# The closing step of a feed-forward: two weight units by token tiles in place of four

## The chip, the cores and the metric

One NeuronCore of one Trainium2 chip. The metric is the device time of one execution in microseconds; lower is better.

## The reference, cut to what matters

A block of two layers, each a mixer and a feed-forward with layer norms, is followed by a second block of another kind. The change touches the feed-forward of both layers of the first block; the second block's input is a modulated form of what the second layer leaves.

```
for l in range(2):
    x = layer_norm(ALPHA * x + mixed, ln1_g[l], ln1_b[l])
    ff = jnp.square(jax.nn.relu(x @ w_up[l])) @ w_down[l]
    x = layer_norm(ALPHA * x + ff, ln2_g[l], ln2_b[l])
...
h = rmsnorm(x, pre_norm_mix) * (1.0 + scale_m) + shift_m
```

x has 256 tokens of 1024 columns, `w_up` is 1024 x 4096, `w_down` 4096 x 1024, all float32.

## The kernel before, in words

The 256 tokens are two token tiles of 128. A weight comes in units of 1 MB. `weight` (from L241) loads a unit from memory into one of two `raw` buffers through the queue of SP (L249); ACT copies it, rounded, into `hi` (L255) and DVE writes the rest, `raw` minus `hi`, into `lo` (L256), in pieces of 1024 columns where nothing else is said. There are four buffers of `hi` and four of `lo`. A `raw` buffer is free again after its last `lo`, a `hi`/`lo` pair after the last matmul that reads it. Each product is three matmuls on PE, hi x hi, hi x lo and lo x hi (`mm3`, L261 to L263).

`layer` holds the feed-forward. `up(j)` computes a block of 512 of the 4096 hidden columns from two units, squares its positive part and splits it into two halves, `hs[j]`. The loop over j then adds the product of `hs[j]` with the `down` units 2j and 2j+1 to four accumulators in PSUM, two token tiles by two halves of 512 columns, with `down` (L285), one unit at a time and both token tiles under it. One `up` runs ahead of it, and in each pass a part of the modulation (`modulation_part`: transfers of `ada` and eight products on DVE, L779), which the second block needs.

The last blocks are done otherwise, so that token tile 0 is ready before tile 1. `downs` (L292) takes several units for one token tile: all but the last unit for both column halves, then the last unit for the first half and for the second. Behind it `close` (L644) does the layer norm of that token tile on DVE: the sum with x (L652), statistics (L329, L331), the root by POOL (L309) and small column work (L310 to L316), the normalized x (L360, L362). In the first layer `split_t` turns x by PE transposes (L340) into `xT` (L345 on ACT, L346 on DVE), which the next layer's mixer reads: its first matmuls are those of `conv_in`, token tile by token tile (L261 to L263, 128x256), with a bias row that SP loads (L474). In the second layer `close` is followed by `modulated` (from L887): a sum of squares on ACT (L892), a scaling on DVE (L896), transposes on PE, gain and shift on DVE and ACT (L905, L903), and the split into `xT`. The second block's first projection (128x496, 24 matmuls a token tile) and two units of a gate (48 matmuls a token tile) read that. `modulation_end`, ahead of the second layer's closing step, sums the modulation parts on PE (L792), finishes them on DVE (L795, L798) and turns them by a PE transpose (L800).

The code gives no order across engines. A scheduler writes, when the program is built, one fixed order for each engine and for the queue of SP; each of them works through its own in turn.

Of the kernel before, what the change touches and what calls it, by code (L numbers as in the profile page):

```python
# [198 lines left out]
class Kernel:  # L199
# [500 lines left out]
    def layer(self, l):  # L700
        nc, vec, act, a = self.nc, self.nc.vector, self.nc.scalar, self.a
        order, ws = self.mixer_ops(l)

        g, b = self.row(a["ln1_g"], D * l), self.row(a["ln1_b"], D * l)
        xT = self.pair("xT", [128, KD, S])
        for t in range(NT):
            acc = [self.acc(), self.acc()]
            self.downs(acc, [(self.mixT, (2 * i, 2 * i + 1)) for i in order], ws, t)
            self.close(t, acc, None, g, b, xT)
        self.dump(f"x1_{l}", self.x[0])  # L710


        def relu2(p, shape):
            r = self.new("t2", shape)
            act.activation(r, p, AF.Relu)
            vec.tensor_tensor(out=r, in0=r, in1=p, op=OP.mult)
            return r

        def up(j):
            h = self.new("mh", [128, 2, 4, S], F32R)  # L720
            ws = [self.weight("up", l, 2 * j + u) for u in range(2)]
            if j == 0:
                for t in range(NT):
                    p = self.mm((128, 512))
                    for u in range(2):
                        self.tok_unit(ws[u], xT, p[:, 256 * u:256 * u + 256], t)
                    self.split_t(relu2(p, [128, 512]), (h[:, 0], h[:, 1]), 0, t)
            else:
                for u in range(2):
                    p = self.mm()  # L730
                    self.ws_unit(ws[u], xT, p)
                    self.split(h[:, 0, 2 * u:2 * u + 2, :], h[:, 1, 2 * u:2 * u + 2, :], relu2(p, [128, 2, 256]))
            return h[:, 0], h[:, 1]

        acc = [[self.acc(), self.acc()] for _ in range(NT)]
        hs = [up(0)]
        for j in range(6):
            hs.append(up(j + 1))
            self.modulation_part(6 * l + j)
            for i in range(2):  # L740
                w = self.weight("down", l, 2 * j + i)
                for t in range(NT):
                    self.down(acc[t], hs[j], (2 * i, 2 * i + 1), w, t, j == 0 and i == 0, False)
        hs.append(up(7))
        g, b = self.row(a["ln2_g"], D * l), self.row(a["ln2_b"], D * l)
        last = l + 1 == DEPTH
        if last:
            self.modulation_end()
        self.xT = self.pair("xT", [128, KD, S])
        ws = [self.weight("down", l, 12 + i) for i in range(4)]  # L750
        for t in range(NT):
            self.downs(acc[t], [(hs[6 + i // 2], (2 * (i % 2), 2 * (i % 2) + 1)) for i in range(4)], ws, t, False)
            self.close(t, acc[t], ALPHA, g, b, None if last else self.xT)
            if last:
                self.modulated(t, 0, 8, self.xT)
        self.dump(f"x2_{l}", self.x[0])
# [659 lines left out]
```

## Time and profile before

| | us |
|---|---|
| runs, lowest / median / highest | 1262.32 / 1267.88 / 1270.29 |
| the profiled execution | 1262.89 |
| its span, first to last instruction | 1261.1 |

The mean granted clock of TensorE over the span is 0.990 of full speed. Times in the rows are counted from the start of the span. PE is TensorE, DVE is VectorE, ACT is ScalarE, POOL is GpSimd, SPq is the queue of SyncE. In a timeline a row is: start, length, engine, line, operation, output and inputs, count; in brackets the idle time of that engine just before, and what ended it. Matmuls are pipelined, so the length of one is more than its distance to the next.

### The profile page before, as it was taken

How to read it: one execution, taken by the hardware profiler on the slowest of the kernel's cores; microseconds unless marked ns; L12 is line 12 of the kernel's file. 1: busy time of each engine (PE TensorE's matmuls, PEld its weight loads, DVE VectorE, ACT ScalarE, POOL GpSimd, SP SyncE). 2: the span in 40 equal slices, each digit the busy share in tenths (PEclk: the TensorE clock that was granted, in tenths of full speed). 3: DMA queues.
4: the chain of work that ended last, by engine and by line, in shares of the span. 5: the costliest groups of instructions: out<-in, count | busy, mean ns of one | idle time of the engine just before them, and what ended most of it. 6: DMA issues, size and time to landing. Idle time of an engine off the chain costs nothing.

```text
span 1261.1 us, 20407 instructions
## 1 busy us (share of the span) xinstructions
PE 1197.4 (95%) x8047; PEld 1061.4 (84%) x8047; DVE 939.6 (75%) x1655; ACT 684.3 (54%) x1178; POOL 37.6 (3%) x60
## 2 busy tenths in 40 slices
PE   6997989999999799999998899999999999999997
PEld 5985679899888578899977688799989978899996
DVE  5998587777899767877868974379988887655553
ACT  4546764434454775444435677667767645444341
POOL 2100000000000000000000000000000000000000
PEclk9999899999999999999999999999999999999999
DMA  8743567777652547787644444255654444555450
GB/s 309 264 148 136 177 234 256 258 290 263 223 219 92 183 150 252 272 286 276 246 163 169 148 169 156 79 201 201 214 187 170 165 168 144 191 201 192 178 199 34
DMA packets 53423, 247.80 MB, mean 196 GB/s; under 512 B 5276, under 2 KB 17596, under 8 KB 30544
## 3 DMA queue, kind: packets, MB, share of 16 engines
q1 hardware_dynamic: 52256, 243.22, 54.0%
q0 software_dynamic: 1072, 3.28, 0.8%
q8 instruction: 63, 1.03, 0.3%
q14 instruction: 32, 0.26, 0.1%
HBM read 241.06 MB, written 6.47 MB: 196 GB/s over the span
## 4 chain that ended last, share of the span: by engine, by line
PE 47%; DVE 23%; DMA 18%; ACT 6%; issue 4%; SPq 0%; POOL 0%; DVEq 0%; ACTq 0%; POOLq 0%
DMA raw<-in_wts 10%; PE mm L263 8%; PE mm L262 8%; PE mm L261 8%; DVE lo L256 8%; DMA s<-in_ada 6%; PE acc L263 5%; PE acc L261 5%; PE acc L262 5%; DVE cy L512 3%; ACT hi L255 3%; DVE t L779 3%; DMA rel<-reld 2%; DVE mask L1022 1%; PE tr L340 1%
## 5 line engine op out<-in xcount | busy, mean ns | idle before, releaser
L256 DVE TENSOR_TENSOR lo<-raw,hi 128x1024 fp32r<-128x1024 f32 (+1 forms) x367 | 430.8, 1185 | 172.4 <-ACT hi L255 171.9
L255 ACT ACTIVATE hi<-raw 128x1024 fp32r<-128x1024 f32 (+1 forms) x367 | 367.2, 1025 | 343.3 <-DMA raw<-in_wts 184.5
L261 PE MATMUL mm<-xT,hi 128*128 128x256 f32 x992 | 281.4, 284 | 0.0
L263 PE MATMUL mm<-xT,lo 128*128 128x256 f32 x992 | 281.0, 283 | 0.0
L262 PE MATMUL mm<-xT,hi 128*128 128x256 f32 x992 | 281.0, 283 | 0.0
L261 PEld LDWEIGHTS mm<-xT,hi 128*128 128x128 f32 x992 | 190.3, 192 | 0.9 <-issue 0.2
L262 PEld LDWEIGHTS mm<-xT,hi 128*128 128x128 f32 x992 | 190.2, 192 | 0.8
L263 PEld LDWEIGHTS mm<-xT,lo 128*128 128x128 f32 x992 | 190.2, 192 | 0.1
L261 PE MATMUL acc<-hi,mh 128*128 128x512 f32 x320 | 128.5, 401 | 5.3 <-ACT mh L599 5.3
L263 PE MATMUL acc<-hi,mh 128*128 128x512 f32 x320 | 126.8, 397 | 0.3 <-DVE mh L346 0.3
L262 PE MATMUL acc<-lo,mh 128*128 128x512 f32 x320 | 126.9, 396 | 0.0
L262 PE MATMUL mm<-lo,xT 128*128 128x256 f32 (+1 forms) x288 | 85.3, 296 | 2.1 <-DVE lo L256 2.1
L261 PE MATMUL mm<-hi,xT 128*128 128x256 f32 (+1 forms) x288 | 86.8, 301 | 0.6 <-ACT kmT L468 0.4
L263 PE MATMUL mm<-hi,xT 128*128 128x256 f32 (+1 forms) x288 | 85.7, 298 | 1.2 <-DVE xT L346 1.2
L779 DVE SCALAR_TENSOR_TENSOR t<-s,silu_c,t 128x512 f32<-128x512 f32 x84 | 62.8, 748 | 29.1 <-DMA s<-in_ada 28.7
L263 PE MATMUL mm<-h,lo 128*128 128x256 f32 x288 | 80.9, 281 | 0.0
L261 PE MATMUL mm<-h,hi 128*128 128x256 f32 x288 | 80.9, 281 | 0.0
L262 PE MATMUL mm<-h,hi 128*128 128x256 f32 x288 | 80.9, 281 | 0.0
L261 PEld LDWEIGHTS acc<-hi,mh 128*128 128x128 f32 x320 | 61.2, 191 | 19.3 <-ACT mh L599 6.1
L263 PEld LDWEIGHTS acc<-hi,mh 128*128 128x128 f32 x320 | 60.8, 190 | 14.7 <-issue 1.4
L262 PEld LDWEIGHTS acc<-lo,mh 128*128 128x128 f32 x320 | 61.2, 191 | 12.6 <-issue 1.1
L261 PEld LDWEIGHTS mm<-hi,xT 128*128 128x128 f32 x288 | 54.9, 191 | 5.7 <-issue 1.8
(386 smaller groups left out, 2179.9 us busy)
## 6 DMA issues: line engine op xcount, KB each, us to landing
raw<-in_wts SPq DMA_DIRECT2D x174, 1024.0 KB
s<-in_ada SPq DMA_DIRECT2D x48, 512.0 KB
rel<-reld SPq DMA_DIRECT2D x64, 64.0 KB
bias<-bo SPq DMA_DIRECT2D x16, 256.0 KB
bias<-bias SPq DMA_DIRECT2D x8, 512.0 KB
cr<-cumd SPq DMA_DIRECT2D x8, 512.0 KB
mh<-in_wts SPq DMA_DIRECT2D x3, 1024.0 KB
row<-in_ln_g SPq DMA_DIRECT2D x4, 512.0 KB
```

Source lines behind the costliest of these rows:

```text
L255: nc.scalar.activation(h[:, s], raw[:, s], AF.Copy)
L256: (lo_on or nc.vector).tensor_tensor(out=l[:, s], in0=raw[:, s], in1=h[:, s].bitcast(F32), op=OP.subtract)
L261: t.matmul(out=out, lhsT=l[0], rhs=r[0], start=start, stop=False)
L262: t.matmul(out=out, lhsT=l[0], rhs=r[1], start=False, stop=False)
L263: t.matmul(out=out, lhsT=l[1], rhs=r[0], start=False, stop=stop)
L340: self.nc.tensor.transpose(out=p[:, i, :], in_=x[:, i * 128:i * 128 + 128], identity=self.ident)
L512: vec.scalar_tensor_tensor(out=y, in0=u[:, c, j:j + 256], scalar=tap(j), in1=y, op0=OP.mult, op1=OP.add)
L779: vec.scalar_tensor_tensor(out=acc, in0=w[:, k, :], scalar=s, in1=acc, op0=OP.mult, op1=OP.add)
L1022: vec.scalar_tensor_tensor(out=isc, in0=rl[:, i, :], scalar=self.widx[:, t, h:h + 1], op0=OP.mult, op1=OP.add, in1=self.nadm[:, t, :] if h ...
```

## The change

The loop over j gets a seventh pass, without a part of the modulation. It runs `up(7)` as every pass runs the next `up`, and multiplies `hs[6]` with the units 12 and 13, both token tiles under one unit. The closing step by token tiles keeps the units 14 and 15 alone. The number of loads, splits and matmuls stays. Both layers run this code.

```
-        for j in range(6):
+        for j in range(7):
             hs.append(up(j + 1))
-            self.modulation_part(6 * l + j)
+            if j < 6:
+                self.modulation_part(6 * l + j)
             for i in range(2):
                 w = self.weight("down", l, 2 * j + i)
                 for t in range(NT):
                     self.down(acc[t], hs[j], (2 * i, 2 * i + 1), w, t, j == 0 and i == 0, False)
-        hs.append(up(7))
...
-        ws = [self.weight("down", l, 12 + i) for i in range(4)]
+        ws = [self.weight("down", l, 14 + i) for i in range(2)]
         for t in range(NT):
-            self.downs(acc[t], [(hs[6 + i // 2], (2 * (i % 2), 2 * (i % 2) + 1)) for i in range(4)], ws, t, False)
+            self.downs(acc[t], [(hs[7], (2 * i, 2 * i + 1)) for i in range(2)], ws, t, False)
             self.close(t, acc[t], ALPHA, g, b, None if last else self.xT)
```

The scheduler's order moves with it. DVE, end of the first layer, before: from the last step of tile 0's norm (`cl` are its small columns) to the norm of tile 1.

```order
383 L362 SCALAR_TENSOR_TENSOR x<-x,cl_3508,row 128x512 x2
384 L256 TENSOR_TENSOR lo<-raw,hi 128x1024
385 L346 TENSOR_TENSOR xT<-tr,xT 128x4x128 x2
386 L256 TENSOR_TENSOR lo<-raw,hi 128x1024 x3
387 L652 SCALAR_TENSOR_TENSOR x<-x,acc 128x512
```

Four `lo` stand between the end of tile 0's norm and the start of tile 1's, around tile 0's two `xT`.

DVE, the same place after the change, from the last split of `up(7)` (`mh`) to the start of tile 0's norm:

```order
370 L256 TENSOR_TENSOR lo<-raw,hi 128x1024
371 L346 TENSOR_TENSOR mh<-t_3405,mh 128x512
372 L256 TENSOR_TENSOR lo<-raw,hi 128x1024 x4
373 L652 SCALAR_TENSOR_TENSOR x<-x,acc 128x512
374 L329 BN_STATS cl_3522<-x 128x6
```

Four `lo` now stand ahead of tile 0's norm. Behind tile 0's norm the order after the change goes on with tile 1's:

```order
384 L362 SCALAR_TENSOR_TENSOR x<-x,cl_3532,row 128x512 x2
385 L652 SCALAR_TENSOR_TENSOR x<-x,acc 128x512
386 L256 TENSOR_TENSOR lo<-raw,hi 128x1024
387 L346 TENSOR_TENSOR xT<-tr,xT 128x4x128 x2
388 L652 SCALAR_TENSOR_TENSOR x<-x,acc 128x512
389 L329 BN_STATS cl_3581<-x 128x6 x2
390 L256 TENSOR_TENSOR lo<-raw,hi 128x1024
391 L331 BN_AGGR cl_3584<-cl_3581 128x2
392 L256 TENSOR_TENSOR lo<-raw,hi 128x1024
```

Tile 1's norm now holds four `lo` up to its last step: the three shown and one in its small columns.

DVE, end of the second layer, before: the scaling and the gain of tile 0's `modulated`, then its `xT`, then the norm of tile 1 (`cl`).

```order
728 L896 TENSOR_SCALAR s<-x,md_6607 128x512 x2
729 L256 TENSOR_TENSOR lo<-raw,hi 128x256 x2
730 L905 TENSOR_SCALAR t_6618<-tr,modc 128x128
731 L905 TENSOR_SCALAR t_6631<-tr,modc 128x128
732 L256 TENSOR_TENSOR lo<-raw,hi 128x256
733 L905 TENSOR_SCALAR t_6618<-tr,modc 128x128
734 L905 TENSOR_SCALAR t_6631<-tr,modc 128x128
735 L652 SCALAR_TENSOR_TENSOR x<-x,acc 128x512 x2
736 L346 TENSOR_TENSOR xT<-t_6618,xT 128x4x128
737 L346 TENSOR_TENSOR xT<-t_6631,xT 128x4x128
738 L329 BN_STATS cl_6688<-x 128x6 x2
```

Tile 0's `xT` stands ahead of all of tile 1's norm but its sum.

The same place after the change, from the scaling of tile 0 (L896) to its `xT`; `cl_6697`, `cl_6698` and L362 are tile 1's norm:

```order
735 L360 SCALAR_TENSOR_TENSOR x<-x,cl_6691,row 128x512
736 L312 SCALAR_TENSOR_TENSOR cl_6697<-cl_6695,cl_6696 128x1
737 L256 TENSOR_TENSOR lo<-raw,hi 128x1024
738 L905 TENSOR_SCALAR t_6642<-tr,modc 128x128
739 L905 TENSOR_SCALAR t_6655<-tr,modc 128x128
740 L316 SCALAR_TENSOR_TENSOR cl_6698<-cl_6697,cl_6695 128x1
741 L256 TENSOR_TENSOR lo<-raw,hi 128x1024
742 L905 TENSOR_SCALAR t_6642<-tr,modc 128x128
743 L905 TENSOR_SCALAR t_6655<-tr,modc 128x128
744 L362 SCALAR_TENSOR_TENSOR x<-x,cl_6698,row 128x512 x2
745 L346 TENSOR_TENSOR xT<-t_6642,xT 128x4x128
746 L346 TENSOR_TENSOR xT<-t_6655,xT 128x4x128
```

The whole norm of tile 1 now stands ahead of tile 0's `xT`, with three of the long `lo` of the gate's units in it, and the short `lo` of the projection's units are gone from here; they stand ahead of tile 0's norm.

PE, second layer, before: the transposes of tile 1's `modulated` stand in the gate's matmuls (`mm`), behind all 24 of tile 0's projection.

```order
3988 L262 MATMUL mm<-lo,xT 128x256
3989 L263 MATMUL mm<-hi,xT 128x256
3990 L340 MATMUL tr<-ident,s 128x128 x8
3991 L261 MATMUL mm<-hi,xT 128x256
3992 L262 MATMUL mm<-lo,xT 128x256
```

Tile 0's projection and half of its gate matmuls are done when PE comes to them.

The same transposes after the change, behind nine matmuls of tile 0's projection (`acc`, 128x496):

```order
3948 L262 MATMUL acc<-lo,xT 128x496
3949 L263 MATMUL acc<-hi,xT 128x496
3950 L340 MATMUL tr<-ident,s 128x128 x8
3951 L261 MATMUL acc<-hi,xT 128x496
3952 L262 MATMUL acc<-lo,xT 128x496
```

Fifteen matmuls of tile 0's projection and all 48 of the gate for tile 0 now stand behind tile 1's transposes.

## Rows read from the trace of the kernel before

**Rows 1.** The page, part 4: the chain that ended last, by engine

```profile
PE 47%; DVE 23%; DMA 18%; ACT 6%; issue 4%; SPq 0%; POOL 0%; DVEq 0%; ACTq 0%; POOLq 0%
```

**Rows 2.** Windows: stretch, length, busy us and count per engine, clock, DMA

```profile
309.46:320.37 10.91, 10.91 (x48) 8.83 (x48) 0.00 (x0) 0.00 (x0) 1.00 0.65 230
320.37:331.88 11.51, 11.51 (x96) 11.46 (x95) 0.00 (x0) 0.00 (x0) 1.00 0.75 268
```

**Rows 3.** Timeline of DVE at the end of the first layer

```profile
342.63 0.69 DVE L652 SCALAR_TENSOR_TENSOR x<-x,acc 128x512 f32<-128x512 f32 x1 [1.31 <-PE acc L263]
...
348.94 1.22 DVE L256 TENSOR_TENSOR lo<-raw,hi 128x1024 fp32r<-128x1024 f32 x1
...
354.79 0.69 DVE L652 SCALAR_TENSOR_TENSOR x<-x,acc 128x512 f32<-128x512 f32 x1
...
359.43 1.22 DVE L256 TENSOR_TENSOR lo<-raw,hi 128x1024 fp32r<-128x1024 f32 x1
...
361.77 1.41 DVE L362 SCALAR_TENSOR_TENSOR x<-x,cl,row 128x512 f32<-128x512 f32 x2
```

**Rows 4.** Timeline of PE behind the first layer

```profile
355.95 0.28 PE L261 MATMUL mm<-hi,xT 128*128 128x256 f32 x1
...
362.66 1.29 PE L340 MATMUL tr<-ident,x 128*128 128x128 f32 x8 [0.80 <-DVE x L362]
...
364.97 0.39 PE L263 MATMUL mm<-hi,xT 128*128 128x256 f32 x1 [0.49 <-DVE xT L346]
```

**Rows 5.** Timeline of PE at the end of the second layer

```profile
643.00 1.08 PE L792 MATMUL tr<-modr,t 128*128 128x48 f32 x8 [0.46 <-DMA t<-in_place]
...
647.60 0.29 PE L800 MATMUL tr<-ident,modc 128*48 128x128 f32 x1 [2.31 <-DVE modc L798]
...
668.20 0.49 PE L261 MATMUL acc<-hi,xT 128*128 128x496 f32 x1 [0.49 <-ACT xT L345]
...
679.06 1.06 PE L340 MATMUL tr<-ident,s 128*128 128x128 f32 x8 [0.35 <-DVE s L896]
...
691.40 0.28 PE L261 MATMUL mm<-hi,xT 128*128 128x256 f32 x1
```

**Rows 6.** Timeline of DVE at the end of the second layer

```profile
654.09 0.69 DVE L652 SCALAR_TENSOR_TENSOR x<-x,acc 128x512 f32<-128x512 f32 x1 [5.88 <-PE acc L263]
...
660.80 1.43 DVE L256 TENSOR_TENSOR lo<-raw,hi 128x256 fp32r<-128x256 f32 x4
...
668.35 1.29 DVE L346 TENSOR_TENSOR xT<-t,xT 128x512 fp32r<-128x512 f32 x2
669.55 0.69 DVE L329 BATCH_NORM_STATS2 cl<-x 128x6 f32<-128x512 f32 x1
...
674.53 1.41 DVE L362 SCALAR_TENSOR_TENSOR x<-x,cl,row 128x512 f32<-128x512 f32 x2
...
677.16 0.15 DVE L321 TENSOR_SCALAR md<-md 128x1 f32<-128x1 f32 x1
...
678.42 0.88 DVE L896 TENSOR_SCALAR s<-x,md 128x512 f32<-128x512 f32 x2
```

**Rows 7.** Timeline of SP's queue and of ACT, first layer's end

```profile
340.75 0.33 SPq L249 DMA_DIRECT2D raw<-in_wts  x1
...
350.75 2.01 ACT L255 ACTIVATE hi<-raw 128x1024 fp32r<-128x1024 f32 x2 [0.38 <-PE acc L263]
```

**Rows 8.** Windows: stretch, length, PE, PEld, DVE, ACT, POOL busy, clock, DMA, GB/s

```profile
345.00:346.00 1.00, 1.00 (x6) 0.84 (x5) 0.93 (x4) 0.00 (x0) 0.00 (x0) 1.00 0.01 0
649.00:652.00 3.00, 3.00 (x8) 2.30 (x7) 0.00 (x0) 0.00 (x0) 0.56 (x2) 0.50 0.50 204
437.00:443.00 6.00, 5.40 (x26) 4.00 (x26) 2.15 (x5) 3.16 (x9) 0.00 (x0) 0.50 0.54 189
1030.00:1032.00 2.00, 0.25 (x2) 0.00 (x0) 0.63 (x1) 1.71 (x3) 0.00 (x0) 1.00 1.02 434
425.00:436.00 11.00, 6.20 (x34) 4.20 (x32) 6.97 (x28) 10.43 (x39) 1.38 (x2) 1.00 0.79 246
```

## The prediction, made before the change was run

> **What bounds the kernel now.** I read the page first: the chain of work that ended last lies on PE for 47% of the span, on DVE for 23% and on transfers for 18% [rows 1]. So I looked for the places where PE isn't fed, and for what DVE does there. Away from the layer ends the feed-forward of the first block runs at PE's rate: 48 matmuls of 512 columns start to start take 10.91 us, 0.227 each, and 96 of 256 columns take 11.51 us, 0.120 each [rows 2]. These two prices carry the sum.
>
> Then I read the end of the first layer's feed-forward on DVE. The layer norm of token tile 0 starts at 342.63, when its sums are there, and has its x done at 348.94; that of tile 1 starts at 354.79, its small column work ends at 359.43, its last two long operations start at 361.77 [rows 3]. PE has tile 1's matmuls under tile 0's norm, and the next mixer's convolution matmuls of tile 0 (from 355.95) under tile 1's; it only waits 0.80 and 0.49 us for tile 1 [rows 4]. Here the cover is just long enough.
>
> At the second layer's end, on PE, the modulation's transpose waits 2.31 us for DVE and its matmuls 0.46 us for a transfer; tile 0's modulated input is used from 668.20, tile 1's transposes stand at 679.06, and the first projection of both tiles is over at 691.40 [rows 5]. On DVE nearly everything between 654.09 and 678.42 is back to back: it is the bound there, with norm and modulation of two tiles and the splits (`lo`) of the next weights in one queue [rows 6].
>
> **The change part by part.** No arithmetic goes and none comes: all 96 matmuls of the last four `down` units stay. In each layer the 24 matmuls of tile 1 with units 12 and 13 move from behind tile 0's norm to ahead of it. That costs the norm of tile 0 24 x 0.227 = 5.5 us of start, takes 5.5 us of cover from it (it had 10.9), and gives the hi/lo buffers of units 12 and 13 back before it instead of under it, so that the splits of the next two weights come ahead of the norm.
>
> First layer. On PE, tile 0's sums would be there at 342.63 + 5.5 = 348.1. And DVE's order now has four `lo` ahead of the norm. The raw data of the second of these units is issued at 340.75 and nothing moves any more after 345.0 [rows 7, 8]. Its two copies on ACT (a pair takes 2.01 [rows 7]) and the last `lo` follow. Two `lo` and one short operation take 361.77 - 359.43 = 2.34, so one is 1.16 [rows 3], and the norm starts at 345.0 + 2.0 + 1.2 = 348.2, with PE or just behind it. Its x is done 6.3 later (342.63 to 348.94), at 354.5. PE has run out of matmuls by then, so tile 0's transposes are no longer covered. DVE then does one add of tile 1, one `lo` and the first xT (0.7 + 1.2 + 0.6): the convolution matmuls of tile 0 start at 357.0 instead of 355.95 and are over 48 x 0.120 = 5.8 later, at 362.8. Tile 1's norm, with four `lo` and both xT of tile 0 in its way, needs 4.6 (354.79 to 359.43) + 4 x 1.16 + 1.2, and from there to its own first xT the path norm, transpose, copy, subtract, some 2.6 (without its one `lo`, 361.77 to 364.97 is 2.0; with it 3.2). That is 354.5 + 4.6 + 4.6 + 1.2 + 2.6 = 367.5 against 364.97 [rows 4]: **2.6 us late**, behind a pause of PE of some 3 us. Bounds: 0, if the stretch after it has room, and 5.5, the cover taken.
>
> Second layer. The same 5.5 us are added ahead of the norm, but the 24 matmuls also run while DVE finishes the modulation, so the waits of 2.31 and 0.46 should go [rows 5]. DVE's order has a `lo` of a weight that is only just loaded ahead of the operations that PE's transpose waits for; that new wait lies between 0 and the 2.31 of today, and I take 0.5, nearer to 0, because 5 us more of PE work lie ahead of it. After today's pause the granted clock is 0.50 (1.2 GHz) from 649 to 652, with 8 matmuls in 3.0 us [rows 8]; at full clock they take 1.8, so with its edges the loss that goes is 1.4. The norm then starts at 654.09 + 5.5 - 2.8 - 1.4 + 0.5 = 655.9.
>
> From there to tile 0's first xT is 14.3 us today (654.09 to 668.35), of which 13 short `lo` of 1.43/4 = 0.36 are 4.7 [rows 6]; these are done ahead of the norm now. But the new order puts the norm of tile 1 into the modulation of tile 0: today that norm, from its statistics at 669.55 to its end at 674.53 + 1.41, is 6.4, less the 2.2 of `lo` in it; and three long `lo`, 3.5. So 14.3 - 4.7 + 4.2 + 3.5 = 17.3, and tile 0's xT comes at 673.2 against 668.35. PE, whose matmuls of tile 1 end at 655.9 + 1.4 + 5.5 = 662.8 (six of 512 columns stand between the norm's first sums and the tile's end), gets tile 0's first projection at 673 instead of 668.20. Tile 1 gains by it: xT of tile 0 (1.3), one `lo` (1.2), then 677.16 to 678.42 (1.3) and 0.6 to its transposes: 677.5 against 679.06. But in PE's order these transposes stand after 9 of the 24 matmuls of tile 0's projection, and behind them queue the other 15, all 48 matmuls of the gate and the 24 of tile 1: 1.06 + 15 x 0.227 + 48 x 0.120 + 0.5 + 24 x 0.227 = 16.2. So the projection ends at 693.7 against 691.40 [rows 5]: **2.3 us late**. Bounds: -4.2, the waits and the half clock that go with nothing late behind, and 5.5.
>
> The clock. Three places of the trace are weighed here: PE stood still for 2.31 us at 645.3 and the clock was 0.50 from 649 to 652; from 425 to 436 PE was busy for 6.2 of 11 us and the clock was 0.50 from 437 to 443; from 1030 to 1032 PE was busy for 0.25 us and the clock stayed at 1.00 [rows 5, 8]. So a pause of two to three us may or may not cost, and a fall lasts 3 to 6 us and doubles the price of what PE does in it. The Trainium skill, "TensorE: Matmul & The Clock Gate" (section "Why this matters for your kernels"), warns against idle gaps of PE between bursts of matmuls, because the clock goes back to half. By that rule each new pause costs, and the sum would be at least the two late starts and 1.5 a layer; by the stretch at 1030 alone it would be the late starts and nothing more. The trace leaves it open at this length. With new pauses of 3 us in the first layer and two of 4 to 6 us in the second, the cost lies between 0 and 3 us a layer (half of 6); I take 1.5 each, half the time in the shorter fall: **3 us**.
>
> The other queues. SP issues one weight ahead of a row load in the first layer; the row waits for its buffer anyway. The position bias in the second layer's mixer has some operations exchanged; I put it at 0 +- 2, since their number doesn't change. The half clock and the two late starts add up to 2.6 + 2.3 + 3.0 = +7.9. The profiled execution took 1262.89 us with a span of 1261.1; so 1270.8 on its scale, or +0.63%. The median of the runs is 1267.88, and on that I state the time: 1276.
>
> **Rivals.**
> *The waits that go are the whole effect.* If the late starts find room behind them, the second layer keeps its -4.2 and the first costs about 1: 1262.9 - 3.2 = 1259.7, or 1264.7 on the median's scale. For it: the next weights are split earlier at both ends, and the waits removed are on PE itself. Against it: DVE has no gap between 654 and 678, and its operations only change places.
> *The first layer's delay dies in the second mixer.* From 425 to 436 PE is busy for 6.2 of 11 us but ACT for 10.43 [rows 8]. If a transfer that is issued regardless ends last there, only the second layer's 2.3 + 1.5 count: 1266.7, or 1271.7. Against it: ACT's work there comes from the same mixer, which starts late.
> *The half clock stays.* Place: the convolution of tile 1 in the first layer, and in the second everything from 673 to past 684. Price: 3.0 (half of 6 us) in the first; in the second, after the nine matmuls that a wait hides, the transposes and 15 matmuls at double price, +4.4; and if the modulation's transpose waits as long as today, the 0.5 becomes 2.3, +1.8. 4.9 + 3.0 + 4.4 + 1.8 = 14.1: 1277.0, or 1282, slower by 1.1%. It decides once PE spends over some 15 us of work at 0.50 that it does at 1.00 today: (12.6 - 4.9) x 2. For it: the fall of 6 us at 437. Against: PE has dense work right after both pauses.
>
> **How the numbers follow.** The forecast has 0.42, the waits alone 0.20, the delay that dies 0.13, the half clock that stays 0.22; 0.03 is left for a gain that I can't name. A measurement of this kernel can tell about 1%, 12.7 us, from no change. Faster by more: 0.03. Slower by more: 0.22 and 0.02 of the forecast's upper end, 0.24. Within: 0.73. The forecast's own range is +3 to +12, 1271 to 1280; with the waits alone at 1264.7 and the half clock at 1282, and some scatter of the median, I give 1263 to 1285.
>
> **What would show it.** In the profile after: a norm of tile 0 that starts about 5.6 us later in the first layer and under 2 us later in the second; no wait over 1 us at the modulation's transpose; a pause of PE of about 3 us ahead of tile 1's convolution; the first projection of tile 0 starting some 4.8 us later against the same moment of up's end, and both tiles' projections done 2.3 us later; new falls to 0.50 behind these pauses. The forecast is wrong if the stretch from the first layer's last up to the taps of the next convolution doesn't grow, if DVE stands idle between the norms, or if PE's pauses at the second end sum to less than today's.

## The result, and the profile after

| | median us (lowest to highest, runs) |
|---|---|
| before, on the same chip | 1264.6 (1255.59 to 1271.58, 20) |
| after | 1273.38 (1265.06 to 1279.77, 20) |
| ratio, 95% interval | 1.0072 (1.0051 to 1.0093) |

The change makes the kernel slower by 0.72%; 0.0072 x 1264.6 is 9.1 us. The profiled execution of after has a span of 1268.3 us and a mean granted clock of 0.977, against 1261.1 and 0.990.

On the page of after, the chain that ended last lies on PE for 49% of the span, on DVE for 21% and on transfers for 18%. It reads like [rows 1]: the page shows no new bound. The loss has to be looked for at the two places of the change. In the views below, rows between those shown are left out.

**A common moment.** Where a feed-forward ends on the span's clock scatters by some us from execution to execution, with the transfers of `ada` ahead of it. So I count from the last split of `up(7)` on DVE, the last thing that both kernels do alike: how long to the last tap of the next convolution in the first layer, and how long to the second block's output projection in the second. The timelines of DVE and PE, before:

```profile
340.64 0.69 DVE L346 TENSOR_TENSOR mh<-t,mh 128x512 fp32r<-128x512 f32 x1
408.75 0.47 DVE L512 SCALAR_TENSOR_TENSOR cy<-u,cols,cy 128x256 f32<-128x256 f32 x1
646.31 0.68 DVE L346 TENSOR_TENSOR mh<-t,mh 128x512 fp32r<-128x512 f32 x1
804.16 0.48 PE L261 MATMUL acc<-hi,act 128*128 128x512 f32 x1
```

and after:

```profile
338.00 0.69 DVE L346 TENSOR_TENSOR mh<-t,mh 128x512 fp32r<-128x512 f32 x1
411.36 0.47 DVE L512 SCALAR_TENSOR_TENSOR cy<-u,cols,cy 128x256 f32<-128x256 f32 x1
649.56 0.68 DVE L346 TENSOR_TENSOR mh<-t,mh 128x512 fp32r<-128x512 f32 x1
814.15 0.48 PE L261 MATMUL acc<-hi,act 128*128 128x512 f32 x1
```

The first stretch grows from 68.11 to 73.36, **+5.25**; the second from 157.85 to 164.59, **+6.74**. Together that is 12.0, more than the 9.1 of the runs: a single execution of each, of which before's was a good one (below). PE isn't tied to this moment: how far it has come with the closing matmuls when DVE does that split differs between executions. Counted from PE's first closing matmul instead (331.88 and 638.50 before, 329.95 and 640.35 after), the stretches grow by 4.5 and 8.1; but that moment scatters more, by up to 3.4 us in layers whose code is unchanged.

**First layer.** DVE's timeline of after, which answers to [rows 3]:

```profile
344.00 2.36 DVE L256 TENSOR_TENSOR lo<-raw,hi 128x1024 fp32r<-128x1024 f32 x2 [2.23 <-ACT hi L255]
346.27 0.68 DVE L652 SCALAR_TENSOR_TENSOR x<-x,acc 128x512 f32<-128x512 f32 x1
```

and PE's, which answers to [rows 4]:

```profile
351.98 1.32 PE L340 MATMUL tr<-ident,x 128*128 128x128 f32 x8 [0.99 <-DVE x L362]
363.35 1.94 PE L340 MATMUL tr<-ident,x 128*128 128x128 f32 x8 [2.60 <-DVE x L362]
```

Tile 0's norm (346.27) starts 8.27 us behind the split of `up(7)`, against 1.99 before: +6.3. It stands right behind the splits of the next weights, which wait 2.23 us for ACT's copies. PE's pause ahead of tile 1's transposes has grown from 0.80 to 2.60 us; these come 25.35 behind the split (22.02 before), and the eight take 1.94 instead of 1.29, since the clock is down, as the next table of windows shows.

**Second layer.** PE's timeline of after, which answers to [rows 5]:

```profile
655.74 0.29 PE L800 MATMUL tr<-ident,modc 128*48 128x128 f32 x1 [2.28 <-DVE modc L798]
672.33 1.94 PE L340 MATMUL tr<-ident,s 128*128 128x128 f32 x8 [4.89 <-DVE s L896]
678.14 0.78 PE L261 MATMUL acc<-hi,xT 128*128 128x496 f32 x1 [3.87 <-ACT xT L345]
698.84 0.28 PE L261 MATMUL mm<-hi,xT 128*128 128x256 f32 x1
```

and DVE's, which answers to [rows 6]:

```profile
650.95 2.71 DVE L256 TENSOR_TENSOR lo<-raw,hi 128x256 fp32r<-128x256 f32 x8 [0.70 <-ACT hi L255]
654.95 0.42 DVE L256 TENSOR_TENSOR lo<-raw,hi 128x256 fp32r<-128x256 f32 x1 [1.18 <-ACT hi L255]
655.29 0.39 DVE L798 SCALAR_TENSOR_TENSOR modc<-modc,cols 128x8 f32<-128x8 f32 x4
660.64 0.69 DVE L652 SCALAR_TENSOR_TENSOR x<-x,acc 128x512 f32<-128x512 f32 x1 [2.49 <-PE acc L263]
687.20 0.69 DVE L346 TENSOR_TENSOR xT<-t,xT 128x512 fp32r<-128x512 f32 x1 [0.32 <-ACT xT L345]
```

The transpose of the modulation still waits 2.28 us: nine short splits of the projection's weights stand on DVE ahead of L798, and for the last of them DVE stands still until ACT has made its copy. Counted from the split of `up(7)`, tile 0's norm starts at 11.08 (before 7.78, +3.3), tile 0's first projection at 28.58 (21.89, +6.7), and both projections are over at 49.28 (45.09, **+4.2**). PE pauses for 4.89 and 3.87 us ahead of tile 0's transposes and of its first projection; the latter pause was 0.49 [rows 5]. Yet the last `xT` of tile 1 is at 37.64 behind the split, no later than before (38.24), as DVE's timeline of before has it:

```profile
684.55 0.69 DVE L346 TENSOR_TENSOR xT<-t,xT 128x512 fp32r<-128x512 f32 x1 [0.59 <-ACT xT L345]
```

What is late is PE's own work for tile 0. Its 24 and 48 matmuls mostly lay under DVE's work for tile 1; now 15 of the 24 and all 48 lie behind tile 1's transposes.

**The clock.** Windows of after: stretch, length, busy us and count of PE, PEld, DVE, ACT, POOL, granted clock, DMA, GB/s:

```profile
363.00:368.00 5.00, 4.65 (x20) 4.22 (x21) 2.25 (x4) 1.20 (x2) 0.00 (x0) 0.50 0.78 253
656.00:659.00 3.00, 3.00 (x9) 2.31 (x8) 2.15 (x8) 1.01 (x4) 1.05 (x2) 0.53 0.60 246
670.00:683.00 13.00, 6.57 (x20) 4.74 (x21) 12.19 (x27) 3.80 (x9) 1.50 (x2) 0.50 0.31 101
708.00:714.00 6.00, 5.53 (x26) 5.14 (x25) 5.63 (x12) 3.96 (x9) 0.00 (x0) 0.50 0.28 90
```

There are four falls to 0.50 (1.2 GHz). Before had the one at 649 to 652 [rows 8], and no other in these stretches.

### The profile page after: what moved, and what is told of

Read it like the earlier page. It is cut to its first block, busy times and chain, and to the rows that moved or that the text cites. A ratio compares the mean times of both kernels' runs of the same rounds, so it can differ in the third digit from the quotient of the medians.

```text
span 1268.3 us, 20410 instructions
## 1 busy us (share of the span) xinstructions
PE 1201.4 (95%) x8047; PEld 1066.7 (84%) x8047; DVE 939.5 (74%) x1655; ACT 684.0 (54%) x1178; POOL 36.6 (3%) x60
## 4 chain that ended last, share of the span: by engine, by line
PE 49%; DVE 21%; DMA 18%; ACT 7%; issue 4%; POOL 0%; SPq 0%; ACTq 0%; DVEq 0%; POOLq 0%
DMA raw<-in_wts 12%; PE mm L261 9%; PE mm L263 9%; PE mm L262 9%; DVE lo L256 8%; PE acc L261 4%; PE acc L263 4%; PE acc L262 4%; DMA s<-in_ada 4%; ACT hi L255 3%; DVE t L779 2%; DVE cy L512 2%; PE tr L340 2%; DMA rel<-reld 2%; DVE mask L1022 1%
## 5 line engine op out<-in xcount | busy, mean ns | idle before, releaser
L261 PE MATMUL mm<-hi,xT 128*128 128x256 f32 (+1 forms) x288 | 88.2, 306 | 0.1
L263 PE MATMUL mm<-hi,xT 128*128 128x256 f32 (+1 forms) x288 | 86.9, 302 | 1.0 <-DVE xT L346 1.0
L261 PE MATMUL mm<-h,hi 128*128 128x256 f32 x288 | 79.6, 276 | 0.0
L262 PE MATMUL mm<-h,hi 128*128 128x256 f32 x288 | 79.6, 276 | 0.0
```

What stands on the lines that cost most here:

```text
L261: t.matmul(out=out, lhsT=l[0], rhs=r[0], start=start, stop=False)
L262: t.matmul(out=out, lhsT=l[0], rhs=r[1], start=False, stop=False)
L263: t.matmul(out=out, lhsT=l[1], rhs=r[0], start=False, stop=stop)
```

## The experiments

Thirteen kernels were timed in all, after among them. "First" and "second" are the two stretches of the section above, from one profiled execution of each, less before's 68.11 and 157.85.

| run | ratio (95%) | first | second |
|---|---|---|---|
| after | 1.0072 (1.0051 to 1.0093) | +5.2 | +6.7 |
| first_only | 1.0034 (1.0011 to 1.0056) | +4.1 | +2.3 |
| second_only | 1.0050 (1.0025 to 1.0076) | +0.6 | +6.7 |
| three_units | 0.9997 (0.9976 to 1.0017) | +1.7 | +2.5 |
| after_gates_late | 1.0073 (1.0036 to 1.0110) | +4.8 | +3.7 |
| before_gates_late | 1.0029 (0.9995 to 1.0063) | -0.3 | +4.0 |
| before_gates_mid | 1.0007 (0.9974 to 1.0041) | +0.8 | -0.4 |
| lo_behind | 1.0091 (1.0060 to 1.0121) | +8.2 | +2.9 |
| tile0_first | 1.0029 (1.0006 to 1.0052) | +4.2 | +6.3 |
| second_t0 | 1.0039 (1.0006 to 1.0071) | -0.3 | +7.9 |
| three_t0 | 1.0037 (1.0004 to 1.0071) | +3.8 | +4.2 |
| after_conv_pool | 1.0072 (1.0045 to 1.0099) | +2.7 | +5.7 |
| warm | 1.0056 (1.0034 to 1.0079) | +3.3 | +7.3 |

In first_only the second layer has before's code, and its stretch is still 2.3 us longer: in that execution the clock fell to 0.50 among the second block's queries (703 to 708), in before's profiled one it didn't. So about 2 us of each number in the last column may be before's good luck. In the first column the four runs with before's code in that layer read -0.3 to +0.8. Each ratio is to runs of before beside it, whose median was between 1264.6 and 1272.2.

**One layer at a time.** The number of closing units is two in one layer and four in the other:

```
+        two = l == 0            # second_only: l == 1
-        for j in range(7):
+        for j in range(7 if two else 6):
...
+        units = range(14 if two else 12, 16)
```

> The two-unit closing step in the first layer alone; the second layer keeps four units. Theory A (lost cover: tile 0's norm starts 5.5 us later and tile 1's convolution waits for its norm) expects what the first layer shows in the trace of the changed kernel and nothing more: the first convolution tap 4 us later against the start of the closing matmuls, a pause of PE of 2 to 3 us ahead of tile 1's transposes, and +4 us in all, a ratio of 1.003. The rival, that the first layer's delay dies in the second mixer, expects the same pause but a ratio of 1.000 and all of the loss in the second layer's run.

> The two-unit closing step in the second layer alone; the first layer keeps four units. Theory A expects both tiles' projections done 5 to 6 us later against the start of the closing matmuls, as in the changed kernel, and +5 us, a ratio of 1.004; with the first layer's run it should add up to the changed kernel's 1.007. If the two ends interact (the second layer's loss exists only because it is entered late), this run is within 2 us of the kernel before, and the two runs' losses do not sum.

Measured: 1.0034 and 1.0050. Of before's 1267.4 us in those runs that is 4.3 and 6.3 us, 10.6 together; after alone is 9.1, and with these intervals the two agree. Each layer costs, and nothing suggests that the two ends interact. The first layer's delay does not die in the second mixer.

In first_only the longest pause lies at another place than in after, ahead of tile 0's transposes. DVE's timeline of first_only, and then PE's:

```profile
347.11 2.36 DVE L256 TENSOR_TENSOR lo<-raw,hi 128x1024 fp32r<-128x1024 f32 x2 [2.38 <-ACT hi L255]
349.38 0.68 DVE L652 SCALAR_TENSOR_TENSOR x<-x,acc 128x512 f32<-128x512 f32 x1
```

```profile
355.09 1.33 PE L340 MATMUL tr<-ident,x 128*128 128x128 f32 x5 [5.44 <-DVE x L362]
```

PE stood idle from 349.65 on (355.09 - 5.44), with all of tile 0's matmuls and most of tile 1's behind it, and the norm shows no wait for PE: it came late because the splits of the convolution's weights stand ahead of it on DVE.

**Three units.** The seventh pass of the loop takes only unit 12; the closing step has 13 to 15.

> Closing step over the last three units in both layers. If the loss follows the cover that tile 0's norm loses, unit by unit, it is half of the change: a ratio of 1.0035. If what costs is the scheduler's new order (splits of the next weights ahead of the norm, tile 1's norm ahead of tile 0's xT), which may stay as before with three units, it is within 1 us of the kernel before: 1.000 to 1.001.

Measured: 0.9997 (0.9976 to 1.0017). Half the cover costs less than half of the loss. PE's timeline of three_units in both layers:

```profile
365.78 1.48 PE L340 MATMUL tr<-ident,x 128*128 128x128 f32 x6 [2.96 <-DVE x L362]
654.12 0.41 PE L801 MATMUL tr<-ident,modc 128*48 128x128 f32 x1 [0.70 <-DVE modc L799]
673.70 1.06 PE L340 MATMUL tr<-ident,s 128*128 128x128 f32 x8 [1.64 <-DVE s L897]
677.29 0.78 PE L261 MATMUL acc<-hi,xT 128*128 128x496 f32 x1 [2.52 <-ACT xT L345]
```

The pauses of both layers are there, smaller in the second. The stretches say +1.7 and +2.5, and of the latter up to 2 may be the queries' clock; that leaves 2 to 4 us, of which the runs allow 2 (0.0017 x 1270). By its own expectation the run falls on the side of the scheduler's order, and that order is indeed mostly the old one here. In the first layer two `lo` stand ahead of tile 0's norm, not four. In the second, one short split stands ahead of the column work that the modulation's transpose waits for, which costs 0.70 us, and on PE tile 1's transposes stand behind all 24 projection matmuls of tile 0, as before. So cover and order shrink together in this run, and it can't tell which of them saves the time. Whether the loss grows with the cover unit by unit or only from a point between three and two isn't settled either.

**The wait at the modulation's transpose.** In two runs the last transpose (L800), its copy and the gate transfers stand on PE behind all closing matmuls, on the changed kernel and on the kernel before; in a third, on the kernel before, behind tile 0's alone:

```
+    def modulation_gates(self):     # L800 to the end of modulation_end, moved here
...
+        if last:                    # before_gates_mid: if last and t == 0, ahead of close
+            with self.tc.issue_after(self.last.ins):
+                self.modulation_gates()
```

> The changed kernel with the modulation's last transpose (L800), its copy and its gate transfers moved behind the last closing matmul in PE's order, so that PE does not stand at 655.7 for 2.28 us while DVE finishes modc. Theory C (the wait that I took as 0.5 and that measured 2.28, with the half clock behind it, is part of the loss) expects the norm of tile 0 to start 2.3 to 3.7 us earlier and the whole to fall by as much: a ratio to the kernel before of 1.004 to 1.005. Theory A with DVE as the bound expects that the norm starts earlier but the projections of the two tiles are done at the same time, because DVE has the same queue to work off: a ratio of 1.007 as for the changed kernel.

> The same move of the modulation's last transpose on the kernel before, where PE waits 2.31 us at it. Theory C expects a ratio of 0.997 to 0.998 (2.3 us of the wait, up to 3.7 with the half clock behind it). Theory A with DVE as the bound at that place expects 1.000: the norm starts earlier, and what DVE has to do before the first projection takes up the time.

> The kernel before with the modulation's last transpose queued on PE behind tile 0's 48 closing matmuls instead of ahead of them, so that neither PE waits 2.3 us for modc nor (as in before_gates_late, where it stood behind all 96) the gate transfers come late. Theory C expects the norm of tile 0 2.3 to 3.7 us earlier and a ratio of 0.997 to 0.998. Theory A with DVE's norm and modulation as the bound, which start with the norm, expects the same; the rival, that later stages wait for something else, expects 1.000.

On the changed kernel the wait is gone and the norm starts 8.40 behind the split of `up(7)` instead of 11.08, 2.7 us earlier. DVE's timeline of after_gates_late, where the norm has no wait at all, and PE's, with the two pauses that follow it:

```profile
667.03 0.68 DVE L652 SCALAR_TENSOR_TENSOR x<-x,acc 128x512 f32<-128x512 f32 x1
```

```profile
678.64 1.94 PE L340 MATMUL tr<-ident,s 128*128 128x128 f32 x8 [6.38 <-DVE s L902]
684.45 0.78 PE L261 MATMUL acc<-hi,xT 128*128 128x496 f32 x1 [3.88 <-ACT xT L345]
```

The first pause takes 1.5 of what the wait gave back, and the second stretch is 3.0 us shorter than after's. The ratio, 1.0073, doesn't show that, but with its interval (0.0037 either way) it can't refuse 3 us either. So the wait costs 2.6 to 3 us in the trace, and its time isn't settled.

On the kernel before, the late version's second stretch is 4.0 us longer (in time 1.0029, with 1 inside the interval): the gate transfers came so late that DVE stood for 4.68 us behind them, a new wait in place of the old one. That this wait makes all of the 4.0 isn't shown. Put behind tile 0's matmuls, the norm starts 1.7 us earlier (6.10 behind the split, from 7.78) and 0.4 us is left of it at the output projection; 1.0007 is no change that can be measured.

**The splits that moved ahead.** The four splits of the convolution's weights go behind tile 0's norm, those of the first projection behind L798. The order alone changes:

```
+        with self.tc.issue_after(self.norm0.ins) if l else ExitStack():
             ws = [self.weight("conv", l, i, ring="mh" if i and l == 0 else None) for i in range(2)]
...
+        with self.tc.issue_after(self.modv.ins):
             ws = [self.weight("first", h, cut=256) for h in range(2)]
```

> The changed kernel with the splits (lo, on DVE) of the next weights kept from moving ahead: in the first layer the four of the convolution stand behind tile 0's norm, in the second those of the first projection behind the modulation's last column work (L798 of the kernel before). Theory C (the splits of weights that have only just come stand ahead of what PE waits for) expects the wait at the modulation's transpose under 0.3 us, no fall of the clock behind it, the norm of tile 0 some 2 to 3.7 us earlier, and a ratio of 1.003 to 1.005. The rival, that DVE has to do these splits before the projection anyway and they only move, expects the waits gone but the projections done at the same time: 1.007.

Measured: 1.0091 (1.0060 to 1.0121), no gain. The wait at the transpose is gone, as theory C said, and the norm starts 6.46 behind the split of `up(7)` instead of 11.08. PE's timeline of lo_behind, second layer:

```profile
683.27 1.94 PE L340 MATMUL tr<-ident,s 128*128 128x128 f32 x8 [7.95 <-DVE s L899]
```

The pause ahead of the transposes grows from 4.89 to 7.95, since the short splits stand in tile 0's norm again, as before the change, but without the matmuls that covered them then. Of the 4.6 us by which the norm is earlier, the second stretch keeps 3.8 (+2.9 against +6.7), but only 1.9 are left at the end of the projections. The first layer pays for it: a new pause of 1.94 us inside tile 0's convolution, for a split, and the longest first stretch of all (+8.2 against +5.2). There DVE has these splits to do at once in any order; the order only chooses what they hold up. The pin of the second layer alone wasn't tried.

The same splits on POOL, in the first layer alone:

```
-        ws = [self.weight("conv", l, i, ring="mh" if i and l == 0 else None) for i in range(2)]
+        ws = [self.weight("conv", l, i, lo_on=nc.gpsimd if l else None, ring="mh" if i and l == 0 else None) for i in range(2)]
```

> The changed kernel with the convolution weights of the second mixer split (lo) on POOL instead of DVE. In the changed kernel these four splits stand on DVE ahead of tile 0's norm in the first layer. If they are a part of the first layer's loss, its norm starts 1.2 us earlier, the pause ahead of tile 1's transposes shrinks by as much and the ratio is 1.005 to 1.006; if only the lost cover counts, 1.007; if POOL is so slow that the convolution waits for its splits, the pause moves ahead of tile 0's convolution and the ratio is 1.008 or more.

Measured: 1.0072, none of the expected gain. The norm starts 4.33 behind the split of `up(7)` instead of 8.27. That is not all the splits' doing, since PE was further ahead at that moment. PE's first closing matmul, in after and then in after_conv_pool:

```profile
329.95 0.40 PE L261 MATMUL acc<-hi,mh 128*128 128x512 f32 x1
```

```profile
332.75 0.40 PE L261 MATMUL acc<-hi,mh 128*128 128x512 f32 x1
```

From there the norm starts 15.19 later instead of 16.32: the splits had cost it 1.1 us in after, close to the 1.2 expected. But the norm becomes longer. DVE's timeline of after_conv_pool, and then POOL's:

```profile
347.94 0.69 DVE L652 SCALAR_TENSOR_TENSOR x<-x,acc 128x512 f32<-128x512 f32 x1 [3.64 <-PE acc L263]
351.07 1.52 DVE L360 SCALAR_TENSOR_TENSOR x<-x,cl,row 128x512 f32<-128x512 f32 x1
352.57 2.79 DVE L360 SCALAR_TENSOR_TENSOR x<-x,cl,row 128x512 f32<-128x512 f32 x1
```

```profile
344.90 9.91 POOL L256 TENSOR_TENSOR lo<-raw,hi 128x1024 fp32r<-128x1024 f32 x4 [170.19 <-ACT hi L255]
354.77 1.00 POOL L309 TENSOR_TENSOR cl<-cl,mhalf 128x1 f32<-128x1 f32 x1
```

Each L360 takes 0.74 in the other runs, here 1.52 and 2.79 while POOL splits; then the norm's root (L309) has to wait for POOL's last split. Tile 0's transposes come 13.45 behind the split of `up(7)` instead of 13.98.

**Tile 0 first.** My theory for the second layer was that tile 1's norm, which now stands ahead of tile 0's `xT` on DVE, makes the loss. Three runs pin the norm and the scaling of tile 1, and the gate's splits, behind tile 0's `xT`: on the changed kernel, on second_only and on three_units.

```
+            if last and t:
+                with self.tc.issue_after(self.pin.ins):   # tile 0's last xT
+                    self.close(t, acc[t], ALPHA, g, b, None)
+                    self.modulated(t, 0, 8, self.xT)
+                continue
...
+            with self.tc.issue_after(self.pin.ins):
                 w = self.weight(nm, i, lo_on=lo_on)
```

> The changed kernel, with DVE's order in the second layer pinned: tile 1's norm and its scaling, and the splits of the gate's units, stand behind tile 0's two xT. Nothing is left out. Theory A (the new order on DVE, tile 1's norm ahead of tile 0's xT, is what costs the second layer its 5 us) expects tile 0's first projection 5 us earlier against the closing step, the two pauses of 4.9 and 3.9 us ahead of it shrunk to one of about 3, and a ratio to the kernel before of 1.003 to 1.005. If DVE's total is the bound, whatever its order, tile 1 comes later by what tile 0 gains: 1.007 as for the changed kernel, or more, because PE then waits for the gate's splits.

> Two units in the second layer alone, as in the run second_only (1.005), with DVE's order there pinned as in tile0_first: tile 1's norm and the gate's splits behind tile 0's two xT. Theory A (DVE's new order makes the second layer's loss) expects xT of tile 0 4 us earlier than in second_only and a ratio of 1.000 (0.998 to 1.002). The rival, for which the trace of tile0_first speaks (tile 0's xT came 4.4 us earlier, tile 1's last xT 5.7 us later, and the output projection's start no earlier), expects the loss to stay: 1.005.

> Three units in both layers (0.9997) with the same pinned order on DVE in the second. If the order pays wherever tile 1's norm has moved ahead, the two pauses of 1.6 and 2.5 us ahead of tile 0's projection shrink and the ratio is 0.997 to 0.999: the best version so far. If tile 1 loses what tile 0 gains, 1.000 or a little above it.

Measured: 1.0029, 1.0039 and 1.0037, against 1.0072, 1.0050 and 0.9997 without the pin. The first looked like a proof, the second is no difference, the third is slower. The traces agree with each other. DVE's timeline of second_t0, whose split of `up(7)` is at 649.60:

```profile
674.64 0.69 DVE L346 TENSOR_TENSOR xT<-t,xT 128x512 fp32r<-128x512 f32 x1 [0.60 <-ACT xT L345]
693.63 0.69 DVE L346 TENSOR_TENSOR xT<-t,xT 128x512 fp32r<-128x512 f32 x1 [0.32 <-ACT xT L345]
```

and PE's waits in the same stretch:

```profile
670.71 1.94 PE L340 MATMUL tr<-ident,s 128*128 128x128 f32 x8 [2.72 <-ACT hi L255]
674.66 0.78 PE L261 MATMUL acc<-hi,xT 128*128 128x496 f32 x1 [2.01 <-ACT xT L345]
689.42 1.07 PE L340 MATMUL tr<-ident,s 128*128 128x128 f32 x8 [2.08 <-DVE s L906]
692.64 0.78 PE L261 MATMUL acc<-hi,xT 128*128 128x496 f32 x1 [2.16 <-ACT xT L345]
```

Tile 0's first `xT` comes at 25.04 behind the split, in second_only at 28.59: 3.6 us earlier. Tile 1's last comes at 44.03 against 37.51: 6.5 later, with four pauses of PE in place of two. In all three pinned runs the stretch to the output projection is as long as without the pin, or longer by 1 to 2 us (-0.4, +1.2, +1.7). So in the traces the order of the two tiles is not the cause; that theory fell. Why the timed runs of tile0_first were some 5 us quicker than after's stays open, since its trace shows no place for it; the two intervals just touch. The pins of the splits and of the tiles' order were tried one at a time, never together.

**The clock alone.** Dummy matmuls fill PE's pauses:

```
+            p = self.acc((128, 2, 256))
+            with self.tc.issue_after(self.last.ins):
+                for _ in range(36):     # 10 behind tile 0's convolution in the first layer
+                    nc.tensor.matmul(out=p, lhsT=hs[7][0][:, 0, 0:128], rhs=hs[7][0][:, 0:2, :], start=True, stop=True)
```

> The changed kernel with 46 dummy matmuls on PE that nobody reads, 36 behind the closing step of the second layer and 10 behind tile 0's convolution in the first, so that PE has no idle pause there and the clock should stay. Theory B (the half clock behind the pauses is the larger part of the loss) expects the granted clock at 1.00 from 669 to 684, tile 1's convolution in 5.8 us instead of 8.1, and a ratio of 1.002 to 1.004. Theory A expects at most 2 us from it: 1.005 to 1.008, since the waits for DVE stay and the dummies may stand in PE's way.

Measured: 1.0056 (1.0034 to 1.0079). Windows of warm, over the same stretches as those of after:

```profile
363.00:368.00 5.00, 4.41 (x26) 3.16 (x25) 3.84 (x6) 1.20 (x2) 0.00 (x0) 1.00 0.96 316
670.00:683.00 13.00, 12.77 (x62) 10.22 (x61) 12.98 (x30) 5.92 (x12) 1.50 (x2) 1.00 0.23 81
```

The clock holds there. From tile 1's transposes to the first tap the first layer takes 12.5 us as against 14.5, 2.0 less. In the second layer I take the moment when the last part of the projection has been read on DVE (L951 of after). DVE's timeline of after:

```profile
705.77 0.18 DVE L951 TENSOR_TENSOR dt<-acc,brow 128x32 f32<-128x32 f32 x1
```

DVE's timeline of warm, with tile 0's norm, and a window of warm ahead of the dummies:

```profile
663.95 0.69 DVE L657 SCALAR_TENSOR_TENSOR x<-x,acc 128x512 f32<-128x512 f32 x1 [3.58 <-PE acc L263]
707.39 0.18 DVE L961 TENSOR_TENSOR dt<-acc,brow 128x32 f32<-128x32 f32 x1
```

```profile
657.00:664.00 7.00, 6.04 (x15) 4.79 (x16) 3.25 (x14) 2.22 (x8) 1.06 (x2) 0.51 0.70 266
```

It is 55.65 behind the split of `up(7)` instead of 56.21, only 0.6 less. But the norm starts 1.1 us later in warm (12.21 behind the split, from 11.08), behind a wait of 2.59 at the modulation's transpose and a longer fall of the clock, which the dummies don't touch. From the norm on it is 43.44 instead of 45.13: **1.7** less, for 13 us at 0.50. Together with the first layer that is 3.7. The ratio gives 0.0016 x 1270 = 2.0, but its interval and after's overlap, and at the output projection warm is no earlier than after (+7.3 against +6.7). So the clock's price is read from these stretches and not shown by the time.

## Why the prediction was right, and where its steps were off

**The time.** Forecast: +7.9 us, +0.63%, slower by less than a measurement of 1% can tell. Measured: +0.72% (0.51 to 0.93). The sign and the sum hold. The stated 1276 stood on 1267.88, the median of three runs of before; on the 20 runs beside after it is 1264.6, where +7.9 gives 1272.5, against 1273.38. One step of the second layer was wrong, and that the sum came out all the same is in part luck.

**First layer, late start 2.6.** The chain came as told: the norm of tile 0 starts 6.3 us later (5.6 foretold), with PE's sums or just behind them by the splits that moved ahead; tile 1's pause is 2.6 us ("some 3"), and its transposes come 3.3 us later behind the split of `up(7)`. "With PE or just behind it" fits after, where the splits held the norm for 1.1 us. It isn't sure to: in first_only, with the same code, PE stood for 5.44 us behind a norm that the splits held up.

**Second layer, late start 2.3.** The step that failed is the new wait at the modulation's transpose, of which I wrote "I take 0.5, nearer to 0, because 5 us more of PE work lie ahead of it". It measured **2.28**, at the upper bound that I had given, and the half clock behind it (656 to 659) came back with it, where I had taken 1.4 off. I had counted one split ahead of L798; there are nine, and the last waits for ACT's copy of a weight that has just landed. In the trace with the transpose moved (after_gates_late) the norm starts 2.7 us earlier. So the norm came 3.3 us later, not 1.8, and tile 0's projection 6.7, not 4.8. From the norm on the forecast fits: 17.5 us to tile 0's first projection (17.3 foretold) and 20.7 from there to the end of both (20.5). But these have the half clock in them, for which the forecast had added another 1.5. So both projections ended 4.2 us later against 2.3 + 1.5 = 3.8, because the missed wait stood in for the clock's term: that is luck. What lies behind the projections, 2.5 us more in the trace, I had put at nothing; some 2 of it may be the queries' clock.

**What lies behind it.** The prediction made two things of the second layer: DVE's new order, and PE's tile 0 work that falls behind tile 1's transposes. In the pinned runs' traces one order of the tiles loses what the other gains. What is left as the cause is the cover: 24 matmuls, 5.5 us, run ahead of a chain of norm, transposes, copies and splits, and PE stands still behind them. This is argued from what the other runs leave over, not shown by a run that takes the cover alone; three_units changes the order as well.

**The clock, 1.5 a layer.** Right in size, as read from the traces of warm and after: 2.0 and 1.7. So in the second layer the other terms behind the norm were some 1.3 too high. The falls aren't alike. In the first layer the convolution of tile 1 is on the path and pays in full; in the second nearly half of the 13 us at 0.50 are idle time of PE, waiting for DVE. The Trainium skill, "TensorE: Matmul & The Clock Gate" (section "Why this matters for your kernels"), warns of idle gaps between bursts of matmuls. Three of after's four falls came behind such gaps (2.60, 2.28 and 4.89 us); ahead of the one among the queries no pause was as long as 1 us.

**The rivals.** "The waits that go are the whole effect" (1264.7): a gain, outside the interval, and the larger wait didn't go. "The first layer's delay dies in the second mixer" (1271.7): refused by first_only (1.0011 to 1.0056). "The half clock stays" (+14.1): the windows of after have 4.65 + 3.00 + 6.57 + 5.53 = 19.8 us of PE's busy time at 0.50, over the 15 of its condition. But the 3.00 don't count, since before was at 0.50 there too, and the 5.53 among the queries are doubtful, since first_only fell there with before's code. That leaves 11.2 to 16.8, so its condition wasn't clearly met. Its clause on the transpose (+1.8) came true. +14.1 would be 1.0112, above the interval.

## What to carry to other kernels

Where an engine's dense work covers another's chain, moving that work ahead of the chain can cost about its whole length, even though nothing is added (here 4.3 and 6.3 us for 5.5 us of cover a layer); none of the orders of the chain's own parts that were tried here made up for it. Ahead of such a step count every instruction that the scheduler puts in front of what the waiting engine needs, with the transfer that the last of them waits for. And where transfers make the span scatter, read a stage from the last event that both kernels share, and keep a second execution of unchanged code as a measure of luck.

## What the runs showed of the hardware that was not expected

- While POOL split four pieces (9.91 us, 2.48 each, where DVE takes 1.2), DVE's L360, with two inputs in SBUF, took 1.52 and 2.79 instead of 0.74. L652 (0.69), which reads an accumulator in PSUM, and the statistics (0.70), with one input, stayed as they were. The Trainium skill, "GPSIMD Engine Reference" (section "1. Specifications"), names operations of VectorE with two SBUF inputs as those that contend with GpSimd; the trace agrees.
- A pause of under 2 us was followed by a fall of the clock in one run and not in another. PE's timeline of tile0_first, first layer, and its windows:

```profile
353.98 1.21 PE L340 MATMUL tr<-ident,x 128*128 128x128 f32 x7 [1.90 <-DVE x L362]
```

```profile
356.00:358.00 2.00, 2.00 (x10) 1.80 (x9) 2.00 (x4) 1.08 (x2) 0.00 (x0) 0.50 0.00 0
```

and those of warm at the same place, ahead of any dummy:

```profile
353.63 1.32 PE L340 MATMUL tr<-ident,x 128*128 128x128 f32 x8 [1.86 <-DVE x L362]
```

```profile
354.00:358.00 4.00, 3.47 (x24) 2.86 (x23) 4.00 (x7) 3.21 (x4) 0.00 (x0) 1.00 0.01 2
```

After 1.90 us the clock fell to 0.50, after 1.86 it stayed at 1.00. In these two runs the length of the pause alone doesn't tell which of the two will come.
